# Three more seven-product pairs in the down projection, thirteen stored units at even distances, and the first conv tap on ScalarE

## The chip, the cores and the metric

The program runs on one core of one Trainium2 chip. The metric is the device time of one execution in microseconds (us). The engines are named as in the profile: PE is TensorE's matmul, PEld its weight load, DVE is VectorE, ACT is ScalarE, POOL is GpSimd, SP is SyncE, which here does nothing but issue DMAs.

## The reference, cut to what matters

One decoder layer over 256 tokens with a model width of 2048, in float32: a combined input projection, two token mixers, a merge, an output projection and a LayerNorm; then the gated MLP with 5632 channels; then a second LayerNorm and a per-layer embedding. The change lies in the MLP and in the projection after it:

```python
def conv_gated_mlp(x, w_gate, w_up, conv_w, conv_b, w_down):
    g = causal_dwconv(x @ w_gate, conv_w, conv_b)   # y_t = sum_j w_j h_{t-2+j} + b
    h = jax.nn.gelu(g) * (x @ w_up)
    return h @ w_down                               # (256, 5632) @ (5632, 2048)
x = layer_norm(ALPHA * x + ffn, ln2_g[i], ln2_b[i])
x = x + jax.nn.sigmoid(x @ w_ple_gate[i]) * (p[i] @ w_ple_proj[i])
```

## The kernel before, in words

**Weights as units.** Every weight matrix is cut into units of 128 x 2048 floats (1 MB), numbered in the order of their use: the MLP has units 136 to 223 (psg n, the gate of block n, is unit 136 + 2n, and psu n, the up projection, is 137 + 2n, for n from 0 to 43), the down projection 224 to 267, the embedding's gate 268 to 283. SP loads a unit in two halves (`raw`, 512 KB, a ring of five buffers, L217). ACT copies each half to float32r (`hi`, L113, a ring of six) and DVE subtracts that from the half (`lo`, L227, a ring of six). A product uses hi and lo of both operands, so float32 accuracy is kept with float32r matmuls. `unit(ahead=3)` prepares the units up to three ahead of the one that PE takes next, in the order of the program. SP's stream is written out by hand in that order and is worked off strictly in turn: an SP instruction that waits holds all that stand behind it. On the other engines the compiler's scheduler orders the instructions, except those that are pinned to the order of the program.

**The MLP.** A block n is two units: 16 steps of a 128x512 and a 128x256 matmul for psg n, then the same for psu n. From psg n comes `gp` (ACT copies a part out of PSUM, DVE adds), the three taps of the convolution (`yc`: the first by a DVE tensor_scalar at L1297, the others by L1302), GELU on ACT (L1303), and the product with `up`. The result is split into hi and lo again and kept in `hC` (one 1 MB buffer for four blocks).

**The down projection** runs in two halves of the output columns (nh 0 and 1). Each half takes 22 units, and each unit is the weights of a pair of blocks. An ordinary unit costs 24 matmuls of 128x512. A unit named in `DN_S` is computed with seven products of half the size in place of eight (21 matmuls), in the manner of Strassen and Winograd. For this it needs four differences of its weight blocks, their splits (`hi_b`, `hi_t` and so on), and sums of the activations. The sums of a pair are formed in the MLP (L756, `hs` L1325), stored to `sd` in DRAM by POOL, and loaded for each half as `hS` by SP.

**Stored differences.** The differences cost four DVE subtractions of 128x512 in a unit (`differences`, L149). For units named in `DN_T` they are formed during the MLP: `park_gen` has SP load the whole unit into a 1 MB buffer `td` (L161), DVE subtract in place, and POOL store it to DRAM (L165). In the down projection SP then loads this back (L179) with the 768 KB of the unit that are needed unchanged. The generator is pulled through 16 steps (a load or a store each) at times spread over n from 6 to 40.

**The buffers.** `td`, `hC`, `hS` and x1T come from one pool of fifteen 1 MB buffers. x1T holds four; hC0 to hC9 take ten, one at every fourth n, the last at n = 36 (hC10 lies elsewhere). From then on to the end of the MLP one buffer is left.

Of the kernel before, what the change touches and what calls it, by code (L numbers as in the profile page):

```python
# [13 lines left out]
AF = mybir.ActivationFunctionType  # L14
ALU = mybir.AluOpType
# [4 lines left out]
P = 128  # L20
# [3 lines left out]
NF = DFF // P  # L24
# [30 lines left out]
WO_C = (0, 2, 4, 6, 7)  # L55

DN_ORDER = (tuple(range(NF // 2)),
            (0, 1, 2, 3, 5, 4, 7, 9, 6, 11, 8, 13, 10, 15, 12, 17, 14, 16, 18, 19, 20, 21))
DN_S = ((1, 3, 5, 7, 9, 11, 13, 15, 17, 19), (1, 3, 5, 7, 9, 11, 13, 15, 17))


WO_T = ((3, 5), (1, 3, 5))
DN_T = ((3, 9, 15, 19), (5, 9, 13, 17))
AFF1 = ((0, 2, 3), (0, 2))
AFF2 = ((0, 2), (0, 2))
LN_ORDER = (1, 0, 3, 2)
# [7 lines left out]
def tile_block(ctx: ExitStack, tc: tile.TileContext, wu, wfv, wpp, xT_in, x_in, pT_in, wlr,  # L74
               chan, gnorm, lng, ident_in, mask_in, cmask_in, out):
    nc = tc.nc
# [20 lines left out]
    def s8(shape, dt=F32, name=None):  # L97
        return big.tile(shape, dt, tag="S8", name=name)

    def t1(name):  # L100
        return sm.tile([P, 256], F32, tag="t1", bufs=6, name=name)

    def t2(name):
        return sm.tile([P, 512], F32, tag="t2", bufs=6, name=name)
# [7 lines left out]
    def copy(o, i, scale=1.0):  # L112
        return nc.scalar.activation(o, i, AF.Copy, bias=0.0, scale=scale)  # L113
# [8 lines left out]
    for _ in range(8):  # L122
# [5 lines left out]
    dn0 = NU - 16 - NF  # L128
    s_units = {b + nh * len(order[nh]) + i
               for b, order, sset in ((52, WO_ORDER, GV_S), (68, WO_ORDER, GR_S),  # L130
                                      (120, OUT_ORDER, WO_S), (dn0, DN_ORDER, DN_S))
               for nh in range(2) for i, n in enumerate(order[nh]) if n in sset[nh]}
    ready = {}

    parked = {b + nh * len(order[nh]) + order[nh].index(n): None
              for b, order, tset in ((120, OUT_ORDER, WO_T), (dn0, DN_ORDER, DN_T))
              for nh in range(2) for n in tset[nh]}
    parked = {u: i for i, u in enumerate(sorted(parked))}
    td = dr.tile([len(parked), P, 2048], F32, name="td")
    sd = dr.tile([len(DN_S[0]), P, 1024], F32, name="sd")  # L140
    hS = {}
# [2 lines left out]
        o = 0 if any(u in r for r in UA) else LO_SHIFT  # L144
        return rlo.tile([P, 1152], F32R, tag="lo", name=f"lo{name}")[:, o:o + 1024]

    def differences(r0, r1, h):
        b12, b11, b22, b21 = r0[:, 0:512], r0[:, 512:1024], r1[:, 0:512], r1[:, 512:1024]
        sub = lambda o, a, b: nc.vector.tensor_tensor(o, a, b, ALU.subtract)  # L149
        if h == 0:  # L150
            sub(b11, b12, b11)
            sub(b12, b12, b22)
        else:
            sub(b22, b22, b11)
            sub(b21, b21, b22)

    def park_gen(units):

        for u, i in [(u, i) for u, i in parked.items() if u in units]:
            w = s8([P, 2048], name=f"td{i}")  # L160
            nc.sync.dma_start(w, wu[u])  # L161
            yield
            for h in range(2):
                differences(w[:, 0:1024], w[:, 1024:2048], h)
            nc.gpsimd.dma_start(td[i], w)  # L165
            yield

    def prep_s(u):


        r0, r1 = [ring.tile([P, 1024], F32, tag="raw", bufs=5, name=f"raw{u}_{h}")
                  for h in range(2)]
        b12, b11, b22, b21 = r0[:, 0:512], r0[:, 512:1024], r1[:, 0:512], r1[:, 512:1024]
        rt = (r0, r1)
        if u in parked:
            nc.sync.dma_start(b11, wu[u, :, 512:1024])
            nc.sync.dma_start(r1, wu[u, :, 1024:2048])
            w = s8([P, 2048], name=f"td{u}")
            nc.sync.dma_start(w, td[parked[u]])  # L179
            rt = (w[:, 0:1024], w[:, 1024:2048])  # L180
# [24 lines left out]
        t2_, t4 = split(rt[1], "t24")  # L205
        ready[u] = [x11, x21, x22, t1_, t3, t2_, t4]
# [48 lines left out]
    chn = cst.tile([P, chan.shape[1]], F32, name="chn")  # L255
# [3 lines left out]
    c_cb = c_cw + 3 * NF  # L259
# [185 lines left out]
    for u in range(8):  # L445
        hi, lo = fvu[u]
        for j in range(2):
# [8 lines left out]
            for t, i, c in seq:  # L456
                o, n = fch[c]
                w, x = prods[t][i]
# [34 lines left out]
    for t in range(2):  # L493
        for c, (o, n) in enumerate(fch):
            n = min(n, 1024 - o)
# [146 lines left out]
    for n in range(16):  # L642
        h, j = n // 2, n % 2
# [368 lines left out]
    mC, mS = {}, {}  # L1012
    fhl = None
    parks = [park_gen(range(120, 136))]
    for n in range(16):
        hi, lo = unit()
# [26 lines left out]
        i = WO_C.index(pair)  # L1043
# [228 lines left out]
    tc.keep_in_program_order(nc.scalar.preload_act_table_set("gelu_apprx_tanh_and_others"))  # L1272
    late.tile([P, GAPS[2]], F32, name="gap2")
    hC = {}
    parks = [park_gen(range(dn0, dn0 + NF))]
    n0 = 6

    def gate_up(name):
        if first:
            return first.pop(0)  # L1280
        hi, lo = unit()
        ps = mmtile(name)
        w_unit(ps, hi, lo, x1T, range(16), True, True)
        return ps

    for n in range(NF):
        psg = gate_up(f"psg{n}")


        g = t2(f"gp{n}")  # L1290
        nc.gpsimd.memset(g[:, 0:2], 0.0)
        comb(psg, g[:, 2:258])
        cw = [chn[:, c_cw + j * NF + n:c_cw + j * NF + n + 1] for j in range(3)]
        for i in range(2):
            nc.gpsimd.tensor_copy(g[:, 258 + i:259 + i], g[:, 129 - i:130 - i])
        y = t1("yc")
        nc.vector.tensor_scalar(y, g[:, 2:258], cw[2], chn[:, c_cb + n:c_cb + n + 1],  # L1297
                                ALU.mult, ALU.add)
        y3 = y.rearrange("p (b n) -> p b n", b=2)
        for j, o in ((1, 1), (0, 0)):  # L1300
            tap = g[:, o:o + 264 - 4 * o].rearrange("p (b n) -> p b n", b=2)[:, :, 0:P]
            nc.vector.scalar_tensor_tensor(y3, tap, cw[j], y3, ALU.mult, ALU.add)  # L1302
        nc.scalar.activation(y, y, AF.Gelu_apprx_tanh, bias=0.0, scale=1.0)  # L1303
        psu = gate_up(f"psu{n}")
        u = t1("up")
        comb(psu, u)
        pair, j = n // 2, n % 2
        if n % 4 == 0:
            hC[n // 4] = (s8 if n < 40 else late.tile)([P, 4, 512], F32R, name=f"hC{n // 4}")
        if pair in DN_S[0]:  # L1310
            if j == 0:
                yp = t2("yp").rearrange("p (k t) -> p k t", t=S)
            h = yp[:, j, :]
        else:
            h = y
        nc.vector.tensor_tensor(h, y, u, ALU.mult)
        dst = hC[n // 4][:, n % 4, :]
        copy(dst[:, 0:256], h)
        nc.vector.tensor_tensor(dst[:, 256:512], h, dst[:, 0:256].bitcast(F32), ALU.subtract)
        if pair in DN_S[0] and j == 1:  # L1320
            v = s_sums(yp)
            for i in range(2):
                w = sm.tile([P, 2, 256], F32R, tag="t2", bufs=6, name="hs")
                copy(w[:, :, 0:P], v[:, 2 * i:2 * i + 2])
                nc.vector.tensor_tensor(w[:, :, P:256], v[:, 2 * i:2 * i + 2],  # L1325
                                        w[:, :, 0:P].bitcast(F32), ALU.subtract)
                nc.gpsimd.dma_start(sd[DN_S[0].index(pair), :, 512 * i:512 * i + 512],
                                    w.rearrange("p i n -> p (i n)").bitcast(F32))
        if n >= 4:
            pull(1)  # L1330
        steps = 2 * sum(map(len, DN_T))
        if n >= n0 and (n - n0) * steps // (NF - 3 - n0) != (n - n0 + 1) * steps // (NF - 3 - n0):
            pull(1, parks)
    while parks:
        pull(1, parks)


    z2 = [None, None]
# [243 lines left out]
```

## Time and profile before

| | |
|---|---|
| time, median of three runs (lowest, highest) | 1662.42 us (1662.34, 1662.45) |
| span of the profiled execution | 1660.7 us |
| PE busy | 1654.7 us |
| DVE, ACT, POOL busy | 1214.7, 938.7, 112.1 us |
| DMA | 414.16 MB, mean 249 GB/s |
| granted TensorE clock, mean | 1.000 |
| MLP's last block ends, down projection starts | 1332.35 us |
| down projection ends | 1558.84 us |

The span goes from the first to the last instruction of one execution; the profiled one is 1.7 us shorter than the median time of a run. Columns of a timeline row are the start, the duration, the engine, the line, the operation with its output and inputs, and in square brackets the idle time of the engine ahead of it with what ended it. Rows of grouped instructions end in "busy us, mean ns of one | idle before". Line numbers are those of the kernel before; in the changed kernel the same instructions have L114 (hi), L254 (lo), L150 (differences), L244 (raw loads), L162 and L168 (td's load and store), L350 (gp), L1323 (the first tap), L1328 (the other taps), L1345 (hC) and L1351 (hs).

### The profile page before, as it was taken

The numbers are of one execution on the slowest core, as the hardware profiler recorded it, in microseconds if no ns is written. First come the engines' busy times: TensorE is split into PE (matmuls) and PEld (weight loads), VectorE is DVE, ScalarE is ACT, GpSimd is POOL, SyncE is SP. The second block draws the span as 40 slices with busy tenths as digits, with TensorE's granted clock in tenths as the row PEclk, the third lists the DMA queues.
The fourth block names the chain that finished last, engine by engine and source line by source line (L and its number), as shares of the span: only waits on it lengthen the run. The fifth ranks groups of instructions, "written<-read, shape, count | busy, mean of one in ns | idle before, by whom it ended". The sixth has DMA issues, their size and how long they took to land.

```text
span 1660.7 us, 24379 instructions
## 1 busy us (share of the span) xinstructions
PE 1654.7 (100%) x8935; PEld 1438.0 (87%) x8935; DVE 1214.7 (73%) x1869; ACT 938.7 (57%) x1355; POOL 112.1 (7%) x262
## 2 busy tenths in 40 slices
PE   9999999999999999999999999999999999999999
PEld 8988888888888888888898888888888888888887
DVE  7644655678876547888987777877777787998774
ACT  6766666765555754455575445555545555556543
POOL 0111111100000110000010010000000000000000
PEclk9999999999999999999999999999999999999999
DMA  8799999986676997878856687777777668798554
GB/s 321 253 253 243 258 263 260 266 233 201 203 224 183 246 251 278 304 247 301 313 175 203 206 291 266 254 240 248 255 250 254 204 227 322 276 359 319 179 187 158
DMA packets 110313, 414.16 MB, mean 249 GB/s; under 512 B 12473, under 2 KB 13761, under 8 KB 104049
## 3 DMA queue, kind: packets, MB, share of 16 engines
q1 hardware_dynamic: 97584, 359.11, 62.7%
q0 software_dynamic: 12608, 53.49, 13.6%
q8 instruction: 70, 1.15, 0.3%
q14 instruction: 51, 0.41, 0.1%
HBM read 388.43 MB, written 24.13 MB: 248 GB/s over the span
## 4 chain that ended last, share of the span: by engine, by line
PE 98%; DMA 1%; DVE 0%; ACT 0%; POOL 0%; SPq 0%; issue 0%; POOLq 0%
PE dn L799 11%; PE psu L294 10%; PE psg L294 9%; PE psm L294 7%; PE pg L340 5%; PE psu L296 5%; PE psg L296 5%; PE gv L799 4%; PE wo L799 4%; PE psm L296 4%; PE psa L294 4%; PE dn_p L799 3%; PE gr L340 3%; PE fv L459 2%; PE gr L799 2%; PE psa L296 2%
## 5 line engine op out<-in xcount | busy, mean ns | idle before, releaser
L113 ACT ACTIVATE hi<-raw 128x1024 fp32r<-128x1024 f32 x502 | 528.2, 1057 | 405.1 <-issue 139.2
L227 DVE TENSOR_TENSOR lo<-raw,hi 128x1024 fp32r<-128x1024 f32 x444 | 539.7, 1222 | 214.9 <-ACT hi L113 210.8
L294 PE MATMUL psu<-x1T,hi 128*128 128x512 f32 x688 | 240.5, 392 | 0.0
L294 PE MATMUL psg<-x1T,hi 128*128 128x512 f32 x672 | 234.9, 392 | 0.0
L296 PE MATMUL psu<-x1T,lo 128*128 128x256 f32 x688 | 192.5, 280 | 0.0
L296 PE MATMUL psg<-x1T,lo 128*128 128x256 f32 x672 | 188.0, 280 | 0.0
L294 PE MATMUL psm<-xT,hi 128*128 128x512 f32 x512 | 181.2, 397 | 0.0
L294 PEld LDWEIGHTS psu<-x1T,hi 128*128 128x128 f32 x688 | 129.3, 188 | 27.4
L294 PEld LDWEIGHTS psg<-x1T,hi 128*128 128x128 f32 x672 | 126.2, 188 | 26.8
L296 PE MATMUL psm<-xT,lo 128*128 128x256 f32 x512 | 143.4, 280 | 0.0
L296 PEld LDWEIGHTS psu<-x1T,lo 128*128 128x128 f32 x688 | 130.7, 190 | 0.0
L296 PEld LDWEIGHTS psg<-x1T,lo 128*128 128x128 f32 x672 | 127.7, 190 | 0.0
L294 PEld LDWEIGHTS psm<-xT,hi 128*128 128x128 f32 x512 | 96.3, 188 | 19.6
L799 PE MATMUL dn<-hi,hC 128*128 128x512 f32 x400 | 111.4, 390 | 0.0
L296 PEld LDWEIGHTS psm<-xT,lo 128*128 128x128 f32 x512 | 97.3, 190 | 0.1
L294 PE MATMUL psa<-oT,hi 128*128 128x512 f32 x256 | 89.5, 392 | 0.0
L799 PEld LDWEIGHTS dn<-hi,hC 128*128 128x128 f32 x400 | 75.1, 188 | 15.5
L113 ACT ACTIVATE hi_t<-raw 128x1024 fp32r<-128x1024 f32 x40 | 42.5, 1062 | 65.7 <-DVE raw L149 51.1
L113 ACT ACTIVATE hi_b<-raw 128x512 fp32r<-128x512 f32 x66 | 55.2, 841 | 42.7 <-DMA raw<-in_wu_dram 19.9
L223 POOL DMA_DIRECT2D lo<-in_wu_dram x58 | 51.0, 879 | 320.9 <-ACT lo L113 125.6
L296 PE MATMUL psa<-oT,lo 128*128 128x256 f32 x256 | 71.6, 280 | 0.0
L195 DVE TENSOR_TENSOR lo_b<-raw,hi_b 128x512 fp32r<-128x512 f32 x66 | 62.5, 954 | 11.4 <-ACT hi_b L113 11.4
(374 smaller groups left out, 3254.5 us busy)
## 6 DMA issues: line engine op xcount, KB each, us to landing
raw<-in_wu_dram SPq DMA_DIRECT2D x555, 512.0 KB, 5.7
lo<-in_wu_dram POOLq DMA_DIRECT2D x58, 512.0 KB, 8.4
td<-in_wu_dram SPq DMA_DIRECT2D x13, 1024.0 KB, 8.6
td<-td POOLq DMA_DIRECT2D x13, 1024.0 KB, 6.7
td<-td SPq DMA_DIRECT2D x13, 1024.0 KB, 6.8
hS<-sd SPq DMA_DIRECT2D x19, 512.0 KB, 7.5
fvraw<-in_wfv_dram SPq DMA_DIRECT2D x13, 524.0 KB, 6.6
sd<-hs POOLq DMA_DIRECT2D x20, 256.0 KB, 5.5
```

The source lines that it names most:

```text
L113: return nc.scalar.activation(o, i, AF.Copy, bias=0.0, scale=scale)
L195: nc.vector.tensor_tensor(lo, src, hi.bitcast(F32), ALU.subtract)
L223: nc.gpsimd.dma_start(lo, wu[u, :, 1024:2048], accum_op=ALU.add)
L227: i = nc.vector.tensor_tensor(lo, raw, hi.bitcast(F32), ALU.subtract)
L294: nc.tensor.matmul(ps, lhsT=hi[i // 8 if hoff == 0 else 0][:, w0 % 1024:w0 % 1024 + P], rhs=a[:, kt % 4, :], start=first and i == 0, stop= ...
L296: nc.tensor.matmul(ps[:, 256:512], lhsT=lo[i // 8 if hoff == 0 else 0][:, w0 % 1024:w0 % 1024 + P], rhs=a[:, kt % 4, 0:256], start=False, ...
L340: nc.tensor.matmul(bs[j][:, 0:m], lhsT=x, rhs=v[:, o:o + m], start=first and i == 0, stop=last and i == 2)
L459: nc.tensor.matmul(fbk[t][c][:, 0:n], lhsT=x, rhs=w[:, o:o + n], start=kt == 0 and i == 0, stop=kt == 15 and i == 2)
L799: nc.tensor.matmul(ps, lhsT=x, rhs=w, start=todo[id(ps)] == total[id(ps)], stop=todo[id(ps)] == 1)
```

## The change

Three things. First, `DN_S` grows from 10 and 9 pairs to 12 and 10, and `DN_ORDER` for the second half is another. Second, 13 units in place of 8 have their differences stored by the MLP. `park_gen` is no longer pulled there; `park_plan` loads the units at n = 4, 7, ..., 40 and subtracts and stores each two blocks later, with the first subtraction pinned to the program's order. td5 to td17 are these units (td5 to td12 before). Third, the first tap is an ACT activation with a scale and a bias.

```diff
 DN_ORDER = (tuple(range(NF // 2)),
-            (0, 1, 2, 3, 5, 4, 7, 9, 6, 11, 8, 13, 10, 15, 12, 17, 14, 16, 18, 19, 20, 21))
-DN_S = ((1, 3, 5, 7, 9, 11, 13, 15, 17, 19), (1, 3, 5, 7, 9, 11, 13, 15, 17))
+            (0, 1, 2, 3, 5, 4, 6, 7, 8, 10, 9, 11, 12, 13, 15, 14, 16, 17, 18, 19, 20, 21))
+DN_S = ((1, 3, 5, 6, 8, 10, 11, 13, 15, 16, 18, 19), (1, 3, 5, 6, 8, 10, 11, 13, 15, 16))
-DN_T = ((3, 9, 15, 19), (5, 9, 13, 17))
+DN_T = ((3, 6, 8, 11, 13, 16, 19), (3, 5, 8, 10, 13, 15))
+PARK_DN = range(4, 43, 3)
...
+    def park_load(u):
+        w = s8([P, 2048], name=f"td{parked[u]}")
+        nc.sync.dma_start(w, wu[u])
+        return w
+
+    def park_store(u, w, pinned=False):
+        for h in range(2):
+            differences(w[:, 0:1024], w[:, 1024:2048], h, pinned and h == 0)
+        nc.gpsimd.dma_start(td[parked[u]], w)
...
+    def park_plan(units, spots, gap=2):
+        units = [u for u in parked if u in units]
+        loaded = {}
+        def step(n):
+            for u, s in zip(units, spots):
+                if s + gap == n:
+                    park_store(u, loaded.pop(u), True)
+            for u, s in zip(units, spots):
+                if s == n:
+                    loaded[u] = park_load(u)
+        return step
...
-        nc.vector.tensor_scalar(y, g[:, 2:258], cw[2], chn[:, c_cb + n:c_cb + n + 1],
-                                ALU.mult, ALU.add)
+        nc.scalar.activation(y, g[:, 2:258], AF.Identity, scale=cw[2],
+                             bias=chn[:, c_cb + n:c_cb + n + 1])
...
-        steps = 2 * sum(map(len, DN_T))
-        if n >= n0 and (n - n0) * steps // (NF - 3 - n0) != (n - n0 + 1) * steps // (NF - 3 - n0):
-            pull(1, parks)
-    while parks:
-        pull(1, parks)
+        park_step(n)
```

Three places show how this moves instructions.

The first is SP's stream near the end of the MLP. td12 is the last stored unit of the kernel before, td16 and td17 are the last two of the changed one. What a row waits for stands in brackets, as semaphores of queues (DMASW of POOL's DMAs, DMAHW of SP's) and engines. Before:

```order
L217 DMA raw215_1_12778<-in_wu_dram 128x1024 [waits DMAHW2_49,DVE_49]
L161 DMA td12_12825<-in_wu_dram 128x2048 [waits DMASW5_49]
L217 DMA raw216_0_12827<-in_wu_dram 128x1024 [waits DMAHW3_49,DVE_49]
L217 DMA raw216_1_12833<-in_wu_dram 128x1024 [waits DMAHW4_49,DVE_49]
L217 DMA raw217_0_12884<-in_wu_dram 128x1024 [waits DMAHW5_49,DVE_49]
```

In the changed kernel:

```order
L244 DMA raw213_1_12712<-in_wu_dram 128x1024 [waits DMAHW2_49,DVE_49]
L162 DMA td16_12771<-in_wu_dram 128x2048 [waits DMASW5_49,DVE_49]
L244 DMA raw214_0_12773<-in_wu_dram 128x1024 [waits DMAHW3_49,Activation_49]
...
L244 DMA raw219_1_13073<-in_wu_dram 128x1024 [waits DMAHW7_49,DVE_49]
L162 DMA td17_13120<-in_wu_dram 128x2048 [waits DMASW2_49,DVE_49]
L244 DMA raw220_0_13122<-in_wu_dram 128x1024 [waits DMAHW0_49,Activation_49]
```

td16's load stands between the halves of units 213 and 214, td17's between units 219 and 220. DMASW5 is here the landing of td15's store and DMASW2 that of td16's. td12's wait before was for the landing of td11's store.

The second is DVE at the subtractions of td15 and td16 in the changed kernel (units 213 and 219 are psu 38 and psu 41):

```order
L150 TENSOR_TENSOR td15_12422<-td15_12422 128x512 [waits DMASW7_49]
L150 TENSOR_TENSOR td15_12422<-td15_12422 128x512 [waits DVE_49]
L254 TENSOR_TENSOR lo213_1_12716<-raw213_1_12712,hi213_1_12714 128x1024 [waits DMAHW7_49,PE_49,Activation_49]
L150 TENSOR_TENSOR td15_12422<-td15_12422 128x512 [waits DVE_49]
L350 TENSOR_TENSOR gp37_12694<-psg37_12661,tmp_12696 128x256 [waits DMASW2_49,Activation_49]
L150 TENSOR_TENSOR td15_12422<-td15_12422 128x512 [waits DVE_49]
...
L254 TENSOR_TENSOR lo219_1_13077<-raw219_1_13073,hi219_1_13075 128x1024 [waits DMAHW4_49,PE_49,Activation_49]
...
L1351 TENSOR_TENSOR hs_13001<-sums_12992,hs_13001 128x2x128 [waits DMASW7_49,Activation_49]
L150 TENSOR_TENSOR td16_12771<-td16_12771 128x512 [waits DMASW5_49]
L350 TENSOR_TENSOR gp40_13055<-psg40_13022,tmp_13057 128x256 [waits Activation_49]
...
L1328 SCALAR_TENSOR_TENSOR yc_13062<-gp40_13055,chn_112,yc_13062 128x256 [waits DVE_49,Pool_49]
L150 TENSOR_TENSOR td16_12771<-td16_12771 128x512 [waits DVE_49]
```

Rows left out here are the other hs, one more tap (yc) and two more subtractions of td16, all between the rows shown. Around unit 213 the kernel before has no subtraction of a stored unit; td12's begin behind the lo of unit 214's first half.

The third is ACT at the end of the seven-product pairs of the second half. Before, an ordinary unit (262) stood behind the last of them (261):

```order
L113 ACTIVATE hi261_t13_14900<-td261_14888 128x1024 [waits DMAHW4_49,PE_49,Activation_49]
L113 ACTIVATE hi261_t24_14904<-td261_14888 128x1024 [waits DVE_49,PE_49]
L113 ACTIVATE hi262_0_14931<-raw262_0_14929 128x1024 [waits DMAHW6_49,DVE_49,PE_49]
L113 ACTIVATE hi262_1_14937<-raw262_1_14935 128x1024 [waits DMAHW7_49,DVE_49,PE_49]
L113 ACTIVATE fold_15015<-dn1_p1_14330 128x512 [waits PE_49,Pool_49]
L113 ACTIVATE pw10_14965<-praw10_14968 128x1024 [waits DMAHW0_49]
...
L113 ACTIVATE hi263_0_14984<-raw263_0_14982 128x1024 [waits DMAHW3_49,DVE_49]
```

In the changed kernel the last one is unit 262 itself:

```order
L114 ACTIVATE hi262_t13_15020<-raw262_0_15004 128x1024 [waits DVE_49,PE_49,Activation_49]
L114 ACTIVATE pw10_15051<-praw10_15054 128x1024 [waits DMAHW5_49]
L114 ACTIVATE fold_15137<-dn1_p1_14409 128x512 [waits DMASW1_49,PE_49]
L114 ACTIVATE hi262_t24_15026<-raw262_1_15005 128x1024 [waits DVE_49,Activation_49]
L114 ACTIVATE pw10_15051<-praw11_15058 128x1024 [waits DMAHW6_49]
L114 ACTIVATE pTs1_15053<-pTr_15062 128x256 [waits DMAHW7_49]
L114 ACTIVATE pTs1_15053<-pTr_15062 128x256
L114 ACTIVATE hi263_0_15070<-raw263_0_15068 128x1024 [waits DMAHW0_49,Activation_49]
```

fold copies a finished product of the last seven-product unit out of PSUM; pw10 and pTs1 belong to the embedding. Before, both splits of the ordinary unit 262 stood ahead of them; now they stand right among the last splits of the seven-product unit, and unit 263's first split follows them as before.

More of the change, by code (lines that the diff above doesn't have):

```diff
@@ L145, in lo_tile, with differences @@
         return rlo.tile([P, 1152], F32R, tag="lo", name=f"lo{name}")[:, o:o + 1024]
-    def differences(r0, r1, h):
+    def differences(r0, r1, h, pinned=False):
         b12, b11, b22, b21 = r0[:, 0:512], r0[:, 512:1024], r1[:, 0:512], r1[:, 512:1024]
@@ L150, in differences @@
         if h == 0:
-            sub(b11, b12, b11)
+            i = sub(b11, b12, b11)
+            if pinned:
+                tc.keep_in_program_order(i)
             sub(b12, b12, b22)
@@ L155, in differences @@
             sub(b21, b21, b22)
+    def park_load(u):
[6 more added lines that the diff above has]
+        nc.gpsimd.dma_start(td[parked[u]], w)
     def park_gen(units):
-        for u, i in [(u, i) for u, i in parked.items() if u in units]:
-            w = s8([P, 2048], name=f"td{i}")
-            nc.sync.dma_start(w, wu[u])
+        for u in [u for u in parked if u in units]:
+            w = park_load(u)
             yield
-            for h in range(2):
-                differences(w[:, 0:1024], w[:, 1024:2048], h)
-            nc.gpsimd.dma_start(td[i], w)
+            park_store(u, w)
             yield
+    def park_plan(units, spots, gap=2):
+        units = [u for u in parked if u in units]
+        assert len(units) == len(spots), (len(units), len(spots))
+        loaded = {}
[7 more added lines that the diff above has]
+        return step
     def prep_s(u):
@@ L1274, in tile_block @@
     hC = {}
-    parks = [park_gen(range(dn0, dn0 + NF))]
-    n0 = 6
+    park_step = park_plan(range(dn0, dn0 + NF), PARK_DN)
     def gate_up(name):
```

## The prediction

> **What bounds the kernel now.** I read the page's chain of waits first, then the windows by stage, then the timeline of the MLP's last blocks.
>
> ```profile
> span 1660.7 us, 24379 instructions
> PE 98%; DMA 1%; DVE 0%; ACT 0%; POOL 0%; SPq 0%; issue 0%; POOLq 0%
> 1180.00:1280.00 100.00, 100.00 (x579) 88.51 (x578) 79.25 (x125) 51.10 (x77) 8.15 (x34) 1.00 0.72 246
> 1475.00:1500.00 25.00, 25.00 (x112) 20.70 (x112) 19.94 (x21) 15.25 (x17) 0.00 (x0) 1.00 1.01 408
> ```
>
> The columns of the windows are the stretch, its length, the busy time of PE, PEld, DVE, ACT and POOL, the granted clock, the DMA share and GB/s. PE carries 98% of the chain and has no gap in the MLP (row 1180) or in the down projection (row 1475). So time is gained only by taking matmuls away, and lost wherever PE is made to wait. In the MLP the other engines have room: DVE is busy for 79 of 100 us, ACT for 51, DMA moves 246 GB/s. In the second half of down DMA is full, at 408 GB/s.
>
> **What is removed on PE.** Three pairs go from 24 to 21 matmuls each, so nine matmuls of 128x512 go.
>
> ```profile
> 1332.35 5.49 PE dn L799 x24
> 1525.52 33.32 PE dn L799 x147
> 1558.84 1.37 PE pp L340 x6
> ```
>
> One takes 33.32 / 147 = 0.2267 us, and nine take **2.04 us**. If nothing else moved, the span would be 1658.7 and the median 1660.4, since the profiled span is 1.7 below the median of the three runs; that is 0.12%. I call less than 0.2%, 3.3 us, no change, because a measurement of this kernel can tell no less. So the aim itself is too small to be seen, and the sign depends on what PE is made to wait for.
>
> **The first tap on ScalarE.** 44 instructions leave DVE and 44 come to ACT.
>
> ```profile
> L1297 DVE TENSOR_SCALAR yc<-gp,chn 128x256 f32<-128x256 f32 x44 | 18.2, 413 | 1.3
> L1303 ACT ACTIVATE yc<-yc 128x256 f32<-128x256 f32 x44 | 18.4, 418 | 40.6 <-DVE yc L1302 40.6
> L149 DVE TENSOR_TENSOR td<-td 128x512 f32<-128x512 f32 x52 | 35.7, 686 | 16.5 <-DMA td<-in_wu_dram 16.4
> ```
>
> DVE loses 44 x 0.413 = 18.2 us. ACT gains an instruction of the kind of L1303's, same shape, 44 x 0.418 = 18.4. ACT's 49% of idle time in row 1180 covers that, and the tap's result is first wanted by GELU and then by hC, blocks ahead of down: I take 0. Without the cover, if each block passed a tap's 0.42 us on to PE, it would be 18 us; nothing in the rows makes that likely.
>
> **Five more stored units, evenly.** DVE takes 20 more subtractions, 20 x 0.686 = 13.7 us, in place of the 18.2 that left: also 0 on average. Five loads and stores of 1 MB in the MLP's 88 units of 5.55 us (row 1260.08 to 1265.63, below) add 10 MB, about 21 GB/s to 246. What matters is the queue, not the sum. SP works strictly in turn:
>
> ```profile
> 1240.38 19.74 SPq L217 DMA_DIRECT2D raw<-in_wu_dram  x8
> 1260.17 0.42 SPq L161 DMA_DIRECT2D td<-in_wu_dram  x1
> 1262.56 36.71 SPq L217 DMA_DIRECT2D raw<-in_wu_dram  x14
> ```
>
> Here td12's load never held SP: it waited for the store of td11, whose load SP had issued some 45 us earlier. In the changed order td16 (n = 37) waits for td15's store, and td17 (n = 40) for td16's, because hC9 takes the last but one of the fifteen buffers at n = 36. td15 is subtracted and stored only at n = 36. While SP waits, no raw half behind it is loaded, beginning with unit 214 (psg 39), later with unit 220 (psg 42). Ahead of the wait unit 213 is all that is loaded. And SP comes to it early: td12 stood ahead of unit 216's halves and was issued at 1260.17, while that unit (psg 40) started at 1287.8 (below, 5.55 us a unit), 27.6 later. td16 is thus reached about 22 us ahead of psu 38.
>
> When does td15's store land? From the kernel before, the same units stand at these times:
>
> ```profile
> 1260.08 0.39 PE L294 MATMUL psu<-x1T,hi 128*128 128x512 f32 x1
> 1261.31 1.23 DVE L227 TENSOR_TENSOR lo<-raw,hi 128x1024 fp32r<-128x1024 f32 x1 [1.21 <-ACT hi L113]
> 1262.45 0.42 DVE L323 TENSOR_TENSOR gp<-psg,tmp 128x256 f32<-128x256 f32 x1
> 1265.63 0.39 PE L294 MATMUL psg<-x1T,hi 128*128 128x512 f32 x1
> 1265.76 1.06 ACT L113 ACTIVATE hi<-raw 128x1024 fp32r<-128x1024 f32 x1 [0.81 <-PE psu L294]
> 1273.95 0.68 DVE L149 TENSOR_TENSOR td<-td 128x512 f32<-128x512 f32 x1
> 1275.06 0.54 POOL L165 DMA_DIRECT2D td<-td  x1 [11.70 <-DVE td L149]
> ```
>
> psu 37 starts at 1260.08, psg 38 at 1265.63: 5.55 us a unit, so psu 38 (unit 213) at 1271.18 and psg 39 at 1276.72. In the new order the last rows of td15 are lo213_1, a subtraction, gp37, a subtraction. With the lo of row 1261.31 ended at 1262.45, then 0.60, 0.42 and 0.69, DVE is done at 1264.2, **7.0 ahead of psu 38**. POOL issues 0.43 later (1275.06 after 1273.95 + 0.68). From there:
>
> ```profile
> DMA to landing us min/median/max: 5.4/6.6/7.5
> DMA to landing us min/median/max: 7.5/8.6/9.8
> 1268.86 0.69 DVE L149 TENSOR_TENSOR td<-td 128x512 f32<-128x512 f32 x1 [3.23 <-DMA td<-in_wu_dram]
> DMA to landing us min/median/max: 7.5/7.5/7.5
> DMA to landing us min/median/max: 3.6/3.6/3.6
> ```
>
> These are the td stores in the MLP, the td loads there, the first use of td12, the raw half issued behind td12's load (row 1262.56), and a raw half issued at 1270.7 with the queue empty. The store lands 5.8 to 7.9 after DVE's end; I take 6.4. Then SP issues td16 and, 0.1 later, raw214_0 behind it. For the landing of that half the lower bound is 3.6 and the 1 MB ahead of it at 408 GB/s, 2.6, so 6.2. The upper is td's 8.6 plus 1.3, by which the half landed after td12's in the rows (1262.56 + 7.5 against 1268.8): 9.9. I take 7.2, nearer the lower one, because SP's wait has emptied the queue. Then hi 1.1 and lo 1.25.
>
> Stall 1: -7.0 + 6.4 + 0.1 + 7.2 + 1.1 + 1.25 = 9.05 after psu 38's start. PE wants that lo 5.78 after it (one unit and one 128x512 matmul). **3.3 us**, by the bounds 1.7 to 7.5.
>
> Stall 2: hi219_1 takes a buffer of the ring of six from unit 216, three units ahead, so it starts when PE ends that unit, at psu 40's start; row 1265.76 shows such a hi right behind a unit's start. From there to the last subtraction of td16 the new order has hi (to 1.1), lo 1.14, two hs 0.75, four subtractions, gp and two taps between them (2.4 + 0.42 + 1.02, the last one at 0.69): 7.05 after psu 40's start. Now 7.05 + 6.4 + 0.1 + 7.2 + 1.1 + 1.25 = 23.1, and psg 42's lo is wanted at 3 x 5.55 + 0.23 = 16.9. **6.2 us**, by the bounds 4.6 to 10.4. td17 is the last, and its own store holds nothing on SP: 0.
>
> **The clock.** Stall 2 leaves PE idle for about 5 us up to its first half-ready matmul.
>
> ```profile
> 1.19 3.32 PE L123 MATMUL warm_ps<-warm 128*128 128x512 bf16 x8 [1.19 <-DVE warm L120]
> 1658.00:1659.50 1.50, 0.00 (x0) 0.00 (x0) 0.00 (x0) 0.00 (x0) 0.00 (x0) 1.00 0.27 96
> 1659.50:1661.00 1.50, 0.00 (x0) 0.00 (x0) 0.00 (x0) 0.00 (x0) 0.00 (x0) 0.52 0.00 0
> ```
>
> After the last matmul the granted clock holds for these rows' first stretch and falls to 0.52 in the second. At the start eight matmuls of 128x512 took 3.32 us in place of 8 x 0.2267 = 1.81. So a fall costs 1.5 us. I take **1.4** for stall 2 and 0 for the shorter stall 1; bounds 0 to 3. The Trainium skill (TensorE: Matmul & The Clock Gate, Part 1: The HAM clock gate (the "warmup" mystery)) has the clock halved once about 3.4 us have passed in idleness, and full again after as long a busy time; by that rule a stall of 3.3 would stay just free of the price and one of 6.2 pay it, as taken here, and no row before shows it in mid-kernel.
>
> **Down.** Its DMA gains five returned units (1.75 MB in place of 1 MB each) and three hS. The second half had 408 GB/s (row 1475); the new order lets stored units follow one another. I take 0, bounds 0 to 4 (a rival below). At its end the last seven-product pair is now unit 262, with no ordinary unit behind it.
>
> ```profile
> 1521.28 0.39 PE L799 MATMUL dn_p<-hi_b,hC 128*128 128x512 f32 x1
> 1522.44 0.58 ACT L113 ACTIVATE fold<-dn_p 128x512 f32<-128x512 f32 x1
> 1522.92 1.99 ACT L113 ACTIVATE pw<-praw 128x1024 fp32r<-128x1024 f32 x2
> 1524.82 0.71 ACT L113 ACTIVATE pTs<-pTr 128x256 fp32r<-128x256 f32 x2
> 1525.81 1.06 ACT L113 ACTIVATE hi<-raw 128x1024 fp32r<-128x1024 f32 x1 [0.28 <-DMA raw<-in_wu_dram]
> ```
>
> fold waits for the first product of unit 262 on PE, which was a unit earlier before. Behind it ACT has hi262_t24 (1.06), one pw (1.0), two pTs (0.71), and only then hi263_0 (1.06), with lo 1.25 after it. Unit 261's first matmul is the row 1521.28 and fold started 1.16 later, when a first product could be read; unit 262's can't be read sooner, so with 1.1 lo263_0 ends near 1.1 + 0.58 + 1.06 + 1.0 + 0.71 + 1.06 + 1.25 = 6.8. 21 matmuls take 4.76, and the lo is wanted 0.45 later, at 5.2: 1.6, bounds 0 to 2. I take **1.2**, since hi263_0 could be placed a little sooner when hi262_t24 waits for nothing.
>
> **Sum.** -2.04 + 3.3 + 6.2 + 1.4 + 1.2 = +10.1. Span 1670.8, time **1672.5**.
>
> **Rivals.**
>
> *Not slower: the waits starve nobody.* If the store lands and the load comes before PE has used up what is prepared, only the 2.04 counts: 1660.4, no change. It decides at the sum of the two landings: 10.3 us for stall 1 (5.78 + 7.0 less 0.1, 1.1 and 1.25) and 7.4 for stall 2 (16.9 less 7.05 and the same). For it: PE had no gap in row 1180 though DVE waited 3.23 us for a td load. Against it: the rows' least sum is 5.8 + 6.2 = 12.0. A gain of more than 3.3 us has nothing in the rows but a stall in them that isn't there.
>
> *Quick landings.* With 10.3 in sum, stall 1 is gone, stall 2 is 2.9 and the clock holds: -2.04 + 2.9 + 1.2 = +2.1, 1664.5, still no change. For it: the empty queue. Against it: 1.7 under the least sum.
>
> *The clock falls at both stalls* and the landings are 2.1 longer in sum, halfway to the upper bounds (7.9 + 9.9 against 6.4 + 7.2): -2.04 + 5.4 + 8.3 + 2.8 + 1.2 = +15.7, 1678.1. For it: td's load had 8.6. Against it: an emptied queue.
>
> *Down becomes bound by DMA.* A stored unit with its hS asks for 2.36 MB (1.75 and 0.5 of 1,048,576 bytes), two in a row for 4.72 in 2 x 4.76 us, 496 GB/s where the row has 408 as the most: 2.0 us short. Pairs 3 and 5, 8 and 10, 13 and 15 of the second half are such. Against it: three units are prepared ahead, and ordinary units lie between. If two of the three aren't covered, 4 us on top: 1676.5.
>
> **How the numbers follow.** Main case 0.60, with 1667 to 1678 as its own range (its terms don't all lie at one end together); not slower 0.08; quick landings 0.06; clock at both 0.12; down 0.11; faster by over 0.2% 0.03. The predicted time is the main case's. Slower by over 0.2%, above 1665.7, are the main case, both clocks and down: 0.83; the same, the two before: 0.14. The range 1664 to 1679 leaves out not slower, faster and little above.
>
> **What would show it.** PE gaps at the starts of psg 39 and psg 42, ended by lo of raw214_0 and raw220_0, of some 3 and 6 us; SP's rows of td16 and td17 with the raws behind them issued in a lump right after the store's landing; a granted clock under 1.00 behind the second gap alone; a DVE row of lo263_0 late by about 1. PE without gaps at the end of the MLP, or the larger gaps elsewhere in the MLP or in down, would make the prediction wrong. The number of dn matmuls must be 990 in place of 999.

## The result

| | before | changed |
|---|---|---|
| time, median (lowest to highest) of 4 runs, same chip | 1662.43 us (1662.34 to 1663.14) | 1674.09 us (1672.42 to 1674.72) |
| span of the profiled execution | 1660.7 us | 1672.9 us |
| down projection starts | 1332.35 | 1341.56 |
| down projection ends | 1558.84 | 1570.97 |

The changed kernel is slower: the ratio is 1.0069, with a 95% interval of 1.0057 to 1.0081. The predicted 1672.5 is 1.6 us below the median, and the range 1664 to 1679 holds it.

The two starts and ends account for 12.1 of the 12.2 us between the profiled spans. Down starts 9.2 later, so the MLP has lost 9.2. Down itself takes 229.4 us where it took 226.5; without nine matmuls it should take 224.45, so of its 229.41 it has lost 5.0, and it has saved 2.0. What follows down takes the same time in both (101.9 us).

The page of the changed kernel, and its chain of waits in order of time (start, duration, what):

```profile
span 1672.9 us, 24464 instructions
PE 96%; DMA 2%; DVE 1%; ACT 1%; issue 0%; SPq 0%; POOL 0%; DVEq 0%; ACTq 0%; POOLq 0%
1268.79 7.98 DMA raw<-in_wu_dram
1276.80 1.06 ACT hi L114
1277.89 1.24 DVE lo L254
1314.28 0.96 ACT hi L114
1315.26 1.24 DVE lo L254
...
1516.76 10.97 DMA hS<-sd
...
1541.33 0.95 DVE pw L1181
1542.44 0.75 DVE pTs L1186 x2
```

The chain leaves PE twice at the end of the MLP. The first time it goes over a raw half, its hi and its lo. The second time it comes to hi and lo over ScalarE's split for hC (0.42 us from 1313.86), which ended 0.2 us after the raw half had landed (6.3 us after its issue at 1307.78). In the second half of down it goes over an hS load and over the embedding's preparation. Timeline rows of PE, SP, POOL, DVE and ACT at the first two places:

```profile
1277.91 0.49 PE L321 MATMUL psg<-x1T,hi 128*128 128x512 f32 x1 [1.11 <-ACT hi L114]
1279.17 0.39 PE L323 MATMUL psg<-x1T,lo 128*128 128x256 f32 x1 [0.76 <-DVE lo L254]
1315.28 0.49 PE L321 MATMUL psg<-x1T,hi 128*128 128x512 f32 x1 [2.79 <-ACT hi L114]
1316.54 0.58 PE L323 MATMUL psg<-x1T,lo 128*128 128x256 f32 x1 [0.77 <-DVE lo L254]
1268.37 0.33 SPq L162 DMA_DIRECT2D td<-in_wu_dram  x1
1268.79 20.48 SPq L244 DMA_DIRECT2D raw<-in_wu_dram  x12
1307.35 0.33 SPq L162 DMA_DIRECT2D td<-in_wu_dram  x1
1307.78 14.07 SPq L244 DMA_DIRECT2D raw<-in_wu_dram  x10
1264.25 0.54 POOL L168 DMA_DIRECT2D td<-td  x1
1302.89 0.54 POOL L168 DMA_DIRECT2D td<-td  x1 [2.33 <-DVE td L150]
1263.27 0.68 DVE L150 TENSOR_TENSOR td<-td 128x512 f32<-128x512 f32 x1
1301.91 0.68 DVE L150 TENSOR_TENSOR td<-td 128x512 f32<-128x512 f32 x1
1314.19 2.23 ACT L114 ACTIVATE hi<-raw 128x1024 fp32r<-128x1024 f32 x2
```

These are psg 39 and psg 42, the two units that were named. SP issues td16 at 1268.37, 4.1 us after POOL issued the store of td15, and raw halves only behind it; td17 follows td16's store by 4.5. Measured against the starts of the same units before, PE is 2.4 us later behind the first place and 6.9 more behind the second. The brackets of PE's rows show less idle time, 1.1 + 0.8 and 2.8 + 0.8, because the matmul that stands alone between them has a row of 0.49 where one costs 0.23 in a stream. What is called a gap or a loss from here on is counted by the starts: what a unit took beyond its matmuls.

Of those 6.9 the gap is 4.1. The rest is the clock. Windows of the changed kernel (columns as in the prediction; the granted clock is the third number from the end):

```profile
1314.00:1315.00 1.00, 0.00 (x0) 0.00 (x0) 0.43 (x1) 1.00 (x2) 0.00 (x0) 1.00 1.03 418
1315.00:1316.00 1.00, 0.49 (x1) 0.19 (x1) 0.74 (x1) 0.87 (x2) 0.00 (x0) 0.91 1.01 369
1316.00:1317.00 1.00, 0.46 (x2) 0.46 (x3) 1.00 (x2) 0.79 (x2) 0.00 (x0) 0.50 1.02 418
...
1320.00:1322.00 2.00, 2.00 (x8) 1.71 (x7) 1.46 (x2) 0.24 (x1) 0.00 (x0) 0.50 0.93 256
1322.00:1323.00 1.00, 1.00 (x6) 0.86 (x5) 0.00 (x0) 0.00 (x0) 0.00 (x0) 0.68 1.02 315
```

The clock is full through the gap itself, falls to a half just as PE begins again, and comes back at about 1322.6, 6.8 us later. From 1316.5 on PE works through these microseconds without a gap, at half its pace: 2.8 us lost. Behind the first place the clock stays at 1.00.

### The profile page after: what moved, and what is told of

It reads as the page before. It is cut to its first block, busy times and chain, and to the rows that moved or that the text cites. A ratio compares the mean times of both kernels' runs of the same rounds, so it can differ in the third digit from the quotient of the medians.

```text
span 1672.9 us, 24464 instructions
## 1 busy us (share of the span) xinstructions
PE 1658.5 (99%) x8926; PEld 1437.5 (86%) x8926; DVE 1213.9 (73%) x1855; ACT 968.0 (58%) x1409; POOL 122.1 (7%) x271
## 4 chain that ended last, share of the span: by engine, by line
PE 96%; DMA 2%; DVE 1%; ACT 1%; issue 0%; SPq 0%; POOL 0%; DVEq 0%; ACTq 0%; POOLq 0%
PE psu L321 9%; PE psg L321 9%; PE dn L826 9%; PE psm L321 7%; PE pg L367 5%; PE psu L323 5%; PE psg L323 5%; PE gv L826 4%; PE wo L826 4%; PE psm L323 4%; PE psa L321 4%; PE dn_p L826 3%; PE gr L367 3%; PE fv L486 2%; PE gr L826 2%; PE psa L323 2%
## 5 line engine op out<-in xcount | busy, mean ns | idle before, releaser
L114 ACT ACTIVATE hi<-raw 128x1024 fp32r<-128x1024 f32 x496 | 521.5, 1057 | 348.1 <-PE psg L321 73.6
L254 DVE TENSOR_TENSOR lo<-raw,hi 128x1024 fp32r<-128x1024 f32 x438 | 532.0, 1221 | 199.3 <-ACT hi L114 195.8
L826 PE MATMUL dn<-hi,hC 128*128 128x512 f32 x352 | 98.3, 390 | 0.2 <-ACT hi L114 0.2
L114 ACT ACTIVATE hi_b<-raw 128x512 fp32r<-128x512 f32 x72 | 60.6, 842 | 49.7 <-DMA raw<-in_wu_dram 23.3
L222 DVE TENSOR_TENSOR lo_b<-raw,hi_b 128x512 fp32r<-128x512 f32 x72 | 68.2, 952 | 17.6 <-ACT hi_b L114 17.6
L826 PEld LDWEIGHTS dn<-hi,hC 128*128 128x128 f32 x352 | 65.9, 188 | 14.3 <-ACT hi L114 0.7
L367 PE MATMUL pg<-hi,x2T 128*128 128x512 f32 (+1 forms) x256 | 69.7, 380 | 0.0
```

Of the source, the lines that this page charges most:

```text
L254: i = nc.vector.tensor_tensor(lo, raw, hi.bitcast(F32), ALU.subtract)
L367: nc.tensor.matmul(bs[j][:, 0:m], lhsT=x, rhs=v[:, o:o + m], start=first and i == 0, stop=last and i == 2)
L826: nc.tensor.matmul(ps, lhsT=x, rhs=w, start=todo[id(ps)] == total[id(ps)], stop=todo[id(ps)] == 1)
```

## The experiments

Times are compared with runs of the kernel before on the same chip, 1662.2 to 1662.3 as a median in each group.

**The wait shortened: subtract and store one block after the load.**

```diff
-    def park_plan(units, spots, gap=2):
+    def park_plan(units, spots, gap=1):
```

> Subtractions and store come one block after the load in place of two; nothing else differs from the changed kernel. Theory (SP stands at the loads of td16 and td17 until the store of the one before has landed): td15's and td16's subtractions are some 11 us earlier, more than the 2.4 and 4.3 us for which PE stood, so both gaps and the slow clock behind the second go: down starts at 1332.4 in place of 1341.6, time 1674.1 - 9.2 = 1664.9 (1664 to 1666), still 2.5 above the kernel before because down itself took 229.4 in place of 226.5. Rival (ScalarE's new tap, or the traffic of five more stored units, starves PE at the end of the MLP): the gaps stay, 1672 to 1675.

Measured: 1664.29 (1663.74 to 1666.03), ratio to before 1.0014 (1.0005 to 1.0023). Down starts at 1332.1 in place of 1341.6. SP still waits at the last two loads for the stores ahead of them, but for 16.7 us in sum in place of 37.1, and PE never stands.

**The wait taken away by other places for the same thirteen loads.**

```diff
-PARK_DN = range(4, 43, 3)
+PARK_DN = range(4, 30, 2)
```

> The thirteen loads stand at n = 4, 6, ..., 28 in place of 4, 7, ..., 40, when more than one of the large buffers is left. Theory: no load waits for a store just issued, so the same as with the earlier subtractions, 1664.9 (1664 to 1666). Rival (it is the denser DMA traffic that matters): the stored units now come closer together, so the gaps move to the middle of the MLP and the time stays at 1670 or above.

Measured: 1664.26, ratio 1.0014 (1.0005 to 1.0023). Down starts at 1332.5.

**The wait lengthened: three blocks after the load.**

```diff
-    def park_plan(units, spots, gap=2):
+    def park_plan(units, spots, gap=3):
```

> Subtractions and store come three blocks after the load. Theory: SP's two waits grow. By the order td15's subtractions end about 6 us later against psu 38 and td16's 3 to 4 later against psu 40: gaps of about 8 and 8 in place of 2.4 and 4.3, with the clock falling twice (2.5 each, one more than now): 1674.1 + 6 + 3.5 + 2.5 = 1686 (1681 to 1690). Rival (the wait is not what starves PE): unchanged, 1674.

Measured: 1686.01, ratio 1.0145 (1.0130 to 1.0160). PE's rows at the same two units:

```profile
1284.42 0.80 PE L321 MATMUL psg<-x1T,hi 128*128 128x512 f32 x1 [7.79 <-ACT hi L114]
1285.68 0.58 PE L323 MATMUL psg<-x1T,lo 128*128 128x256 f32 x1 [0.47 <-DVE lo L254]
1327.22 0.79 PE L321 MATMUL psg<-x1T,hi 128*128 128x512 f32 x1 [6.59 <-ACT hi L114]
1328.48 0.58 PE L323 MATMUL psg<-x1T,lo 128*128 128x256 f32 x1 [0.47 <-DVE lo L254]
```

The gaps are at the same two units, 7.8 and 6.6 us before their first matmul, and the clock is at a half behind both. With the same instructions and the same bytes, one number moves the loss in the MLP from nothing (one block) over 9.2 (two) to 20.7 (three). The windows of the end of the MLP, of the kernels with one block and with the early places:

```profile
1250.00:1332.00 82.00, 82.00 (x475) 72.53 (x474) 64.74 (x102) 44.33 (x71) 8.45 (x30) 1.00 0.73 259
```

```profile
1250.00:1332.00 82.00, 82.00 (x475) 72.49 (x474) 58.67 (x91) 45.06 (x72) 5.43 (x27) 1.00 0.58 195
```

PE is busy for all of the 82 us in both. With one block DMA moves 259 GB/s there, where the changed kernel moved 234 from 1260 to 1279 and 237 from 1279 to 1316, and PE doesn't wait: it was not the traffic. This settles the MLP's part.

**The first tap back on VectorE.**

```diff
-        nc.scalar.activation(y, g[:, 2:258], AF.Identity, scale=cw[2],
-                             bias=chn[:, c_cb + n:c_cb + n + 1])
+        nc.vector.tensor_scalar(y, g[:, 2:258], cw[2], chn[:, c_cb + n:c_cb + n + 1],
+                                ALU.mult, ALU.add)
```

> The changed kernel with the first tap back on VectorE. Theory (the tap is covered on either engine): within 1.5 us of the changed kernel, 1674.1, rather above it, since one tap of 0.41 us now stands on VectorE between td16's subtractions. Rival (ScalarE is late because of the 44 taps): 3 us or more faster.

Measured: 1674.61 (1672.52 to 1677.90), ratio 1.0077 (1.0061 to 1.0094), not to be told from the changed kernel. In its profile PE stands at the same two places, 1.4 + 0.8 and 2.7 + 0.8 us by its rows, but the clock falls behind both, for 3.4 us each (the last section comes back to this). The tap itself is seen better further on, where no stall hides it.

**What is left in down: early places, and the embedding's preparation three units later.** With the MLP clean the kernel is still 2.1 us slower than before. In the profile of the early places PE has gaps in the second half of down of 0.4 at unit 257, 0.9 at 260 and 1.8 at 262 and 263.

```diff
-    down(1, 2, {4: lambda: load_z2(1), 8: late_loads, 14: lambda: pq.append(ple_prep(1))})
+    down(1, 2, {4: lambda: load_z2(1), 8: late_loads, 17: lambda: pq.append(ple_prep(1))})
```

> On the kernel with the early stored units (1664.26): the preparation of the embedding (two pw, two pTs on ScalarE, as many on VectorE, three loads) comes behind unit 17 of the second half in place of 14, so that hi263_0 follows hi262_t24 directly. Theory (ScalarE's and VectorE's order at the end of the seven-product pairs costs 1.8: 0.7 before the last product of unit 262, which waits for fold, and 1.1 at unit 263, which waits for pw and pTs): the 1.1 goes, 1663.2. Rival (unit 263 is late because its DMA is late): no change, 1664.3.

Measured: 1664.17, ratio 1.0013 (1.0004 to 1.0022): the expected 1.1 did not come. The gap at unit 263 is gone, as the theory had it, but the gap at 262 is now 1.2 in place of 0.7, one of 0.5 stands at 266, where the preparation now is, and the two earlier ones are larger by 0.9. The order was the cause at 263, and moving it only moved the loss.

**The gain loads earlier, and later.** `late_loads` issues two loads of 1 MB. It also has four statistics instructions for VectorE, but the compiler's scheduler puts these at the same place in all three kernels (from 1452 to 1459), so that only the loads move.

```diff
-    down(1, 2, {4: lambda: load_z2(1), 8: late_loads, 14: lambda: pq.append(ple_prep(1))})
+    down(1, 2, {4: lambda: load_z2(1), 5: late_loads, 14: lambda: pq.append(ple_prep(1))})
```

> On the kernel with the early stored units (1664.26): the two gain loads of 1 MB each, which take DMA time in the densest stretch of the second half, come behind unit 5 in place of 8. Theory (the 1.3 us of gaps at units 257 and 260 are DMA's: it runs at about 420 GB/s there and the halves land late): most of it goes, 1663.0, if the three units in between have 2 MB to spare. Rival 1 (DMA is full there too): the gap moves ahead, 1664.3 or up to 2 more. Rival 2 (the gaps come from the order on VectorE and ScalarE): no change.

Measured: 1662.52 (1661.51 to 1663.42), ratio 1.0002 (0.9993 to 1.0011). The gaps at 257 and 260 are gone, and 1.2 us remain, all at 262 and 263. The 2 MB came where DMA had room: from 1470 to 1481 it moves 425 GB/s, in place of the early kernel's 340.

```diff
-    down(1, 2, {4: lambda: load_z2(1), 8: late_loads, 14: lambda: pq.append(ple_prep(1))})
+    down(1, 2, {4: lambda: load_z2(1), 11: late_loads, 14: lambda: pq.append(ple_prep(1))})
```

> The same with the two gain loads behind unit 11, so behind td259 and ahead of unit 260's halves. Theory (DMA is full from unit 255 to 262): the gap at unit 257 goes (0.4), the ones at unit 260 grow by up to 4.9 us, the time that these 2 MB take at 420 GB/s: 1664 to 1669. Rival (the order on the engines): no change, 1664.3.

Measured: 1665.06, ratio 1.0016 (1.0007 to 1.0025): 257 is clean and unit 260 costs 4.2 us, in the direction that was expected of DMA. About 1.7 of it is the clock, by the estimate that half of the 3.4 us is lost for which it was at a half (last section). Windows of the changed kernel, and of the one with the gains behind unit 5:

```profile
1490.00:1508.00 18.00, 18.00 (x81) 14.90 (x80) 10.51 (x11) 8.41 (x9) 0.00 (x0) 1.00 1.02 416
1508.00:1546.00 38.00, 34.82 (x147) 26.80 (x146) 31.60 (x34) 23.33 (x26) 0.00 (x0) 1.00 0.81 297
```

```profile
1500.00:1508.00 8.00, 8.00 (x37) 6.63 (x36) 5.87 (x7) 6.16 (x7) 0.00 (x0) 1.00 0.87 292
1508.00:1533.00 25.00, 24.45 (x106) 19.47 (x105) 21.05 (x23) 15.98 (x19) 0.00 (x0) 1.00 0.87 328
```

In the changed kernel DMA is full for 18 us at 416 GB/s, PE eats what is prepared, and the gaps come when it is eaten. Two megabytes at 420 GB/s are 5.0 us of that stretch. But the traffic is not all of it: behind the full stretch SP waits from 1502.3 to 1511.5 for a ring buffer that, by the profile, VectorE's subtractions of unit 257 still need. DMA moves 152, 23 and 0 GB/s in the three microseconds from 1509, and the hS load in the chain above, which unit 260 waits for, is issued at 1516.76 only. So the gap at unit 260 again stands behind a wait of SP.

**Both moves.**

> Gain loads behind unit 5 and the embedding's preparation behind unit 17, on the early stored units. If both theories hold, 1664.26 - 1.3 - 1.1 = 1661.9, and only the 0.7 at unit 262 is left: between the kernel before (1662.2) and the 1660.2 that nine matmuls less would make of it.

Measured: 1662.15, ratio 1.0000 (0.9991 to 1.0009), with 2.3 us of gaps in down, 1.2 of them at unit 262.

**The fold two units later**, on the kernel with both moves:

```diff
-            if pair in sset and not set(order[i + 1:]) & set(sset):
+            last = max(k for k, p in enumerate(order) if p in sset)
+            if i == last + (2 if (nm, nh) == ("dn", 1) else 0):
                 fold()
```

> On the kernel with early stored units, gain loads behind unit 5 and the embedding's preparation behind unit 17 (1662.15; 2.1 us of gaps in down, 1.2 of them at unit 262, 0.6 at 260, 0.35 at 266): the fold of the last seven-product unit is written two units later, so that its copy on ScalarE no longer stands ahead of hi262_t24. Theory (fold waits for PE's first product of the same unit and holds the split that this unit needs): the 1.2 goes, 1660.9. Rival (unit 262's halves land late): no change, 1662.2.

Measured: 1661.61 (1660.55 to 1667.24), ratio 0.9997 (0.9988 to 1.0006). The gap at 262 is gone entirely, so fold was its cause. 0.8 remain at unit 266, where VectorE has the fold's additions between the last splits:

```profile
1547.02 0.68 DVE L847 SCALAR_TENSOR_TENSOR z<-z,fold 128x512 f32<-128x512 f32 x1
1547.63 1.22 DVE L254 TENSOR_TENSOR lo<-raw,hi 128x1024 fp32r<-128x1024 f32 x1
1548.76 0.68 DVE L848 TENSOR_TENSOR fold<-fold,dn_p 128x512 f32<-128x512 f32 x1
```

```profile
1548.90 0.50 PE L826 MATMUL dn<-lo,hC 128*128 128x512 f32 x1 [0.52 <-DVE lo L254]
```

**The last seven-product pair given up**, on the kernel with the gains behind unit 5: `DN_S[1]` without 16.

> On the kernel with early stored units and gain loads behind unit 5 (1662.52; 1.2 us of gaps in down, all at units 262 and 263): the last seven-product pair of the second half, 16, is computed with 24 matmuls again. Theory (the end gap comes from a seven-product unit with no ordinary one behind it before the embedding's preparation): the 1.2 goes and three matmuls, 0.7, come back: 1662.0. Rival (the gap is that of unit 263's loads): it stays, 1663.2.

Measured: 1661.64, ratio 0.9996 (0.9988 to 1.0005). The end gap is gone with three matmuls back; 0.5 us of gaps are left, at 260.

**All ten pairs kept, the last one a unit earlier.**

```diff
-            (0, 1, 2, 3, 5, 4, 6, 7, 8, 10, 9, 11, 12, 13, 15, 14, 16, 17, 18, 19, 20, 21))
+            (0, 1, 3, 2, 5, 6, 4, 8, 7, 10, 11, 9, 13, 12, 15, 16, 14, 17, 18, 19, 20, 21))
```

> On the same kernel (1662.52): the second half's order is 0, 1, 3, 2, 5, 6, 4, 8, 7, 10, 11, 9, 13, 12, 15, 16, 14, 17, ..., so that all ten seven-product pairs stay and the last stands at unit 261 with an ordinary one behind it, as before the change. Theory (order at the end): the 1.2 goes, 1661.3, faster than both kernels. Rival (DMA, denser now that the stored units come one place earlier): gaps of up to 3 us in the middle of the half, 1663 to 1665.

Measured: 1664.67, ratio 1.0017 (1.0008 to 1.0026). The rival's price came: 4.0 us of gaps, most of them in the middle of the half. That they are DMA's is shown in part. Ahead of the gap at 1484.6 ScalarE waits 6.0 us for a raw half, and DMA moves 417 GB/s from 1485 to 1496. The chain to the gap at 1499.6 goes over a td load of 13.6 us, but then over VectorE's subtractions, with DMA at 143 GB/s from 1496 to 1501.

**The tap once more, where no gap hides it**: the kernel with the late fold, with the tap on VectorE.

> The kernel with the late fold (1661.61), with the first tap back on VectorE. Here PE stands for less than 1 us in down and not at all in the MLP, so what the tap is worth is no longer hidden behind the gaps. Theory (covered on either engine): 1661.6, within 0.5. Rival (13 stored units only fit into VectorE's time in the MLP because its 44 taps left): gaps of the MLP's splits, 1663 or above.

Measured: 1661.13 (1660.20 to 1662.40), ratio 0.9994 (0.9985 to 1.0003). The tap is worth nothing that can be told, on either engine. PE has no gap in down in this run's profile.

No kernel here is faster than the one before by more than the runs can tell. The best two medians, 1661.1 and 1661.6, are 1.2 and 0.7 below it. The span with the late fold is 0.9 shorter than before, 1659.8 against 1660.7: 2.0 saved on matmuls less about 1.0 of gaps left in down.

## Why the prediction was right, and where not

**Nine matmuls, -2.04.** Right. In the run just above, the late fold with the tap on VectorE, down has no gap and takes 224.5 us: 226.5 less 2.0.

**The tap, 0.** Right. Its price on ScalarE was mis-sized:

```profile
L1323 ACT ACTIVATE yc<-gp,chn 128x256 f32<-128x256 f32 x44 | 26.3, 598 | 43.2 <-DVE gp L350 43.2
```

598 ns in place of the 418 of L1303's GELU of the same shape, 26.3 us in place of 18.4; ScalarE's idle time covers it all the same.

**The two waits of SP.** Right in place, cause and order; the loads, the store and the halves behind them stand where the text had put them. td15's last subtraction ended at 1263.95, 7.1 ahead of psu 38 (predicted 7.0), and td16's 6.9 behind psu 40's start (predicted 7.05, though the terms listed for it add up to 6.9 as well). The sizes were 2.4 and 4.1 in place of 3.3 and 6.2, and the term that was too large is the landings. From the end of the last subtraction to SP's issue of the next load passed 4.4 and 4.8, where I took 6.4 and had 5.8 for the least: POOL's td15 store landed 4.1 us after its issue, in place of 5.4 to 7.5, because with SP standing nothing else was under way: DMA moved 255 GB/s in these 4.1 us, 1.05 MB, which is the store alone. The raw half behind the td load took 8.0 and 6.3 from its own issue, where 7.2 was taken. The condition of the rival "quick landings" was 10.3 in sum; the sums were 12.4 and 11.1, with 0.4 between the two issues where I had 0.1, so it was nearer than its 0.06 said for the second stall, and both gaps stayed.

**The clock, 1.4.** It fell at the second gap and not at the first, as predicted, but that was partly luck, and the size was too small: 2.8. The reason given was the length of a stall, and that is not what decided. With the tap on VectorE the first stall was hardly longer, 1.4 + 0.8 us by PE's rows in place of 1.1 + 0.8, and the clock fell there too. I had priced a fall by the warm-up matmuls, whose slow stretch is about 3 us long; here it was 6.8. The Trainium skill (TensorE: Matmul & The Clock Gate, Part 1: The HAM clock gate (the "warmup" mystery)) has the clock halved after an idle window of about 3.4 us and full again after a busy one, with windows that run free of the kernel. The slow stretch agrees, it is two such windows long; but PE's longest idle stretch was 2.8 us, so a wholly idle window was not needed. The last section works this out.

**Down's middle, 0, with bounds 0 to 4.** Here the prediction's value failed, and its rival named why: "Down becomes bound by DMA". 3.2 us were lost at units 257 and 260, and moving 2 MB out of the densest stretch took the gaps away on the early kernel, where they were 1.4. That DMA fills the stretch was read from the row of 408 GB/s; I let the three units prepared ahead cover it, without adding up what they have to cover. The gains' 2 MB, which stood unchanged in the program and unmentioned in the prediction, were the part of that sum that decided.

**Down's end, 1.2, with bounds 0 to 2.** Right in place, too small in size: 1.8. Rows of ScalarE in the changed kernel:

```profile
1537.92 0.60 ACT L114 ACTIVATE fold<-dn_p 128x512 f32<-128x512 f32 x1 [1.04 <-PE dn_p L826]
1538.61 1.06 ACT L114 ACTIVATE hi_t<-raw 128x1024 fp32r<-128x1024 f32 x1
1539.58 1.04 ACT L114 ACTIVATE pw<-praw 128x1024 fp32r<-128x1024 f32 x1
1540.53 0.71 ACT L114 ACTIVATE pTs<-pTr 128x256 fp32r<-128x256 f32 x2
1541.14 1.99 ACT L114 ACTIVATE hi<-raw 128x1024 fp32r<-128x1024 f32 x2
```

fold waits for PE, then come hi262_t24, pw and pTs, and only then unit 263, in the predicted order. What the text missed is that hi262_t24 itself is late by the same wait: 0.7 of the 1.8 fell within unit 262.

**The sum.** -2.0 + 2.4 + 4.1 + 2.8 + 3.2 + 1.8 = 12.3 against the predicted -2.0 + 3.3 + 6.2 + 1.4 + 0 + 1.2 = 10.1. The waits were put 3.0 too high, the clock, down's middle and its end 5.2 too low. That the total is near is luck: these errors run against each other.

**What stays open.** The gaps in down's middle are 3.2 in the profile of the changed kernel, 3.9 with one block between load and store and 1.4 with the early places, though down's own program is the same. The last two kernels do not differ by that: their medians are 1664.29 and 1664.26, and the profiled execution of the one with one block is the slowest of its ten, 1666.03. So these gaps seem to change by a microsecond or two from one execution to the next, and a single profile sizes them no better. Why they change stays open.

## What to carry to other kernels

In a queue that is worked off strictly in turn, a load whose buffer has to be stored first passes its wait on to everything behind it. Look, for each such load, at how many buffers are left at that moment and at how late the work that frees one stands on its own engine: here one more block of distance cost 9.2 us and the next 11.5, with the same instructions. And where a stage's DMA is full, a saving on PE shortens the time in which the same bytes must come: add up the bytes that come in that stretch, those of unchanged loads too.

## What was not expected of the hardware

The clock fell without a single long gap. In the kernel with the gains behind unit 11, PE stood 0.4, 0.8 and 0.5 us by its rows, with one and then two matmuls between them, and the clock went to a half for 3.4 us:

```profile
1515.60 0.50 PE L826 MATMUL dn<-hi_b,hC 128*128 128x512 f32 x1 [0.39 <-ACT hi_b L114]
1516.86 0.50 PE L826 MATMUL dn<-lo_b,hC 128*128 128x512 f32 x1 [0.76 <-DVE lo_b L222]
1518.13 0.50 PE L826 MATMUL dn<-hi_b,hS 128*128 128x512 f32 x1 [0.54 <-DMA hS<-sd]
...
1518.00:1519.00 1.00, 0.86 (x3) 0.73 (x4) 0.95 (x1) 0.96 (x2) 0.00 (x0) 0.89 1.01 414
1519.00:1520.00 1.00, 1.00 (x4) 0.58 (x3) 1.00 (x2) 0.53 (x1) 0.00 (x0) 0.50 1.04 426
```

In the changed kernel's first stall PE stood 1.1 and 0.8 us with one matmul between, and the clock held. With the tap on VectorE, at the same place, it fell:

```profile
1278.13 0.49 PE L321 MATMUL psg<-x1T,hi 128*128 128x512 f32 x1 [1.36 <-ACT hi L114]
1279.39 0.39 PE L323 MATMUL psg<-x1T,lo 128*128 128x256 f32 x1 [0.76 <-DVE lo L254]
1281.00:1282.00 1.00, 1.00 (x4) 0.86 (x4) 0.97 (x3) 0.83 (x2) 0.00 (x0) 0.50 1.00 336
```

So the length of one idle stretch doesn't tell whether the clock falls. The times of its changes do. A row's granted clock gives the moment (0.91 from 1315 to 1316 is a fall at 1315.8), and the slow stretches come out as 3.4 us (gains behind unit 11, and both with the tap on VectorE), 6.8 (changed kernel) and 10.2 (both with three blocks): one, two and three times 3.41. The two falls with three blocks, at 1279.0 and 1323.4, are 13 times 3.41 apart. So in these runs the clock changes only at marks 3.41 us apart. Where the marks lie differs from one profile to the next: the first rise of the clock comes 4.0 to 7.1 us after the start.

Cut at these marks, PE's idle time by its rows (whose ends are modelled) sorts all the cases. In the piece ahead of a fall it was 1.5 us with the gains behind unit 11, 2.1 and 2.9 with the tap on VectorE, 2.8 in the changed kernel and 2.4 and 2.8 with three blocks. The first stall of the changed kernel is cut by the mark at 1278.3 into 1.1 and 0.8, and the most that left the clock full in any of the profiles was 1.4. A slow clock came back behind a piece with 0.4 us of idle time or less and stayed down behind one with 0.7 or more. The changed kernel had 0.7 in its first slow piece, so it paid for two. The same stall can thus go free in one execution and cost the clock in another.
